# Down-projection: FFN rows loaded from POOL's queue, and the residual added by accumulating DMAs

## The chip, the cores and the metric

The kernel runs on one core of one Trainium2 chip. The metric is the device time of one execution in microseconds; the time before is the median of three runs. The engines are PE (TensorE matmul), DVE (VectorE), ACT (ScalarE), POOL (GpSimd) and SP (SyncE, which only issues DMAs here). Each engine works through its own instructions in the order in which the built program holds them, and waits on semaphores of the others.

## The reference

One step of a decoder layer on 1024 prompt positions and 8 sample tokens, that is 1032 columns in the kernel's layout. Only the end of it bears on the change:

```python
h = x + merged @ w_out
up = rmsnorm(h, norm_ffn) @ w_up
...
gate, val = jnp.split(c, 2, axis=-1)
h = h + (jax.nn.gelu(gate) * val) @ w_down
...
y_prompt = rmsnorm(h_p, norm_final)
y_sample = rmsnorm(h_s, norm_final)
```

`w_down` is 2816 x 1024, so the contraction of the down-projection has 22 row blocks of 128 (`NFF = 22`) and its output has 8 row blocks of 128 (`KT = 8`).

## The kernel before

Everything lies feature by position: a tile has 128 features as partitions and 1032 positions as columns. Matmuls are fp32 by splitting: each operand is a rounded part (`hi`) and a rest (`lo`), and three matmuls (hi x hi, hi x lo, lo x hi) make one product. Casts of the rounded part stand on ACT, the differences on DVE.

**Up-projection.** For each f of 22, `up_unit(f)` (L1263 on) computes two row blocks, `ff_rows(f)` applies the convolution, the gelu and the product and stores the result, g of f, to a scratch tensor `g_d[f]` in device memory from SP's queue (L1324). The residual h was stored to `hT_d` long before.

**Loading a row of g.** `load_g(f, after)` (L1334) makes one FFN row ready for the down-projection. It takes a buffer `gt`; `touch` (L92) copies one element into it on DVE, which ties the load to whatever `after` names; the DMA (L1337) loads 516 KB from SP's queue; ACT casts `gh` (L1340); DVE forms `gl` (L1341).

**Down-projection.** The 22 rows are taken in groups of 4, 5, 5, 5 and 3 (`DOWN_GROUPS`). For each of the first four groups, `down` (L1366) runs over the eight output row blocks j, and for each j over three blocks of columns (384, 384, 264). One such block is a chain of three matmuls per f in one PSUM bank; then `post` evicts it: DVE adds the sum to `hT[j]` (tile name `hD`, L1372). While `wide[0]` is not None, `mmtile` deals the blocks to two PSUM pools of four banks each in turn, so eight banks hold sums that are being made or that wait for their eviction. `hT[j]` before the first group is the residual: `load_h` loads the eight tiles from POOL's queue (L1351), in two steps that run in the last up-projection unit behind the loads of the first group's rows.

**What sets the order.** Steps that are to run beside matmuls are closures in a list `side`; each contraction step calls `tick`, which pops one. The loads of a following group are such steps, each with an `idle` between: while group n is multiplied, the rows of group n+1 are loaded. The language's scheduler then fixes the order of the instructions on each engine when the program is built; nothing moves at run time.

The last group of three rows (`last_down`) and the final normalisation follow; the change does not touch them.

Of the kernel before, what the change touches and what calls it, by code (L numbers as in the profile page):

```python
# [9 lines left out]
F32 = mybir.dt.float32  # L10
# [3 lines left out]
ALU = mybir.AluOpType  # L14
# [6 lines left out]
KT = 8  # L21
S = 1024
NS = 8
T = S + NS
DFF = 2816
NFF = DFF // P
# [18 lines left out]
def kernel(  # L45
# [8 lines left out]
    nc = tc.nc  # L54
# [14 lines left out]
    def uid(s):  # L69
        counter[0] += 1  # L70
        return f"{s}_{counter[0]}"

    def ftile(name, dt=F32):
        return fpool.tile([P, FCOLS], dt, tag="f", name=uid(name))
# [10 lines left out]
    def xtile(name):  # L85
        return pxx.tile([P, 512], F32, tag="xx", name=uid(name))
# [4 lines left out]
    def touch(dst, src):  # L91
        nc.vector.tensor_copy(dst[0:1, 0:1], src[0:1, 0:1])  # L92
# [62 lines left out]
    side = deque()  # L155
# [13 lines left out]
    def drain():  # L169
        while side:  # L170
            side.popleft()()


    def load_raw(w2d, r0, nk, c0):
        raw = wpool.tile([P, KT, P], F32, tag="wraw", name=uid("wraw"))
        nc.sync.dma_start(
            raw[:, :nk, :],
            w2d[r0:r0 + nk * P, c0:c0 + P].rearrange("(k p) c -> p k c", p=P),
        )
        return raw  # L180
# [10 lines left out]
    def split_w(raw, nk):  # L191
        parts = [split_part(raw[:, k:min(k + 4, nk), :]) for k in range(0, nk, 4)]
        hi = [parts[k // 4][0][:, k % 4, :] for k in range(nk)]
        lo = [parts[k // 4][1][:, k % 4, :] for k in range(nk)]
        return hi, lo

    def load_w(w2d, r0, nk, c0):

        return split_w(load_raw(w2d, r0, nk, c0), nk)

    def unit(w, src, nk, post, b, blocks):

        hi, lo = w
        t0, n = blocks[b]
        ps = mmtile("mm")
        for k in range(nk):
            xh, xl = src(k, t0, n)
            nc.tensor.matmul(ps[:, :n], hi[k], xh, start=(k == 0), stop=False)  # L208
            nc.tensor.matmul(ps[:, :n], hi[k], xl, start=False, stop=False)  # L209
            nc.tensor.matmul(ps[:, :n], lo[k], xh, start=False, stop=(k == nk - 1))  # L210
            if k < nk - 1:
                tick(1 / nk)
        post(b, t0, n, ps)
        tick(1 / nk)
# [16 lines left out]
    def dense(w, ahi, alo, post, tbs=(0, 1, 2), blocks=TB):  # L231
        def src(k, t0, n):
            return ahi[k][:, t0:t0 + n], alo[k][:, t0:t0 + n]

        for b in tbs:
            unit(w, src, len(ahi), post, b, blocks)
# [891 lines left out]
    for hp in range(2):  # L1128
        bh = ftile("bh", F32R)
        bl = ftile("bl", F32R)  # L1130
        for hf in range(2):
            ps = xtile("bps")
            for j in range(4):
                nc.tensor.transpose(ps[:, j * P:(j + 1) * P], oA[hp][:, hf * 4 + j, :], ident)
            cs = slice(hf * 512, hf * 512 + 512)
# [27 lines left out]
    for p in range(2):  # L1163
        t0, n = HALF[p]
        for i in range(4):
            h = ftile("hT")
# [5 lines left out]
    hT_d = dpool.tile([KT, P, T], F32, tag="hT_d", name="hT_d")  # L1172
    g_d = dpool.tile([NFF, P, T], F32, tag="g_d", name="g_d")
# [83 lines left out]
    ups = {}  # L1257
# [5 lines left out]
    def up_unit(f):  # L1263

        wa, wb = up_weights(f)
        ups[f] = [ftile("up") for _ in range(2)]
        for up in ups[f]:
            nc.gpsimd.memset(up[:, 0:2], 0.0)

        def outs(p):  # L1270
            t0, n = HALF[p]
            return [up[:, 2 + t0:2 + t0 + 2 * n] for up in ups[f]]

        pair_unit(wa, wb, hn, outs)
# [41 lines left out]
    def ff_rows(f, t0=0, t1=T):  # L1316
        ug, uv = ups.pop(f)
        n = t1 - t0
        cg, cv = (ftile("cv") for _ in range(2))
        conv(f, ug, cg, t0, t1)  # L1320
        nc.scalar.activation(cg[:, :n], cg[:, :n], AF.Gelu_apprx_tanh)
        conv(f + NFF, uv, cv, t0, t1)
        nc.vector.tensor_tensor(cg[:, :n], cg[:, :n], cv[:, :n], op=ALU.mult)
        nc.sync.dma_start(g_d[f][:, t0:t1], cg[:, :n])  # L1324

    for p in range(2):
        t0, n = HALF[p]
# [6 lines left out]
    def load_g(f, after):  # L1334
        gt = ftile("gt")
        touch(gt, after)
        nc.sync.dma_start(gt[:, :T], g_d[f])  # L1337
        gh = ftile("gh", F32R)
        gl = ftile("gl", F32R)
        nc.scalar.copy(gh[:, :T], gt[:, :T])  # L1340
        nc.vector.tensor_tensor(gl[:, :T], gt[:, :T], gh[:, :T].bitcast(F32), op=ALU.subtract)  # L1341
        return gh, gl

    hT = []
    gs = []

    def load_h(js):
        for j in js:
            h = ftile("hD")
            touch(h, ups[NFF - 1][0][:, 2:3])  # L1350
            nc.gpsimd.dma_start(h[:, :T], hT_d[j])  # L1351
            hT.append(h)

    for f in range(EARLY, NFF):
        if f == NFF - 1:
            side.append(idle)
            for i in range(DOWN_GROUPS[0]):
                side.append(lambda i=i: gs.append(load_g(i, ups[NFF - 1][0][:, 2:3])))
            side.append(lambda: load_h(range(4)))
            side.append(lambda: load_h(range(4, KT)))  # L1360
        up_unit(f)
        drain()
        ff_rows(f)


    def down(f0, gs):  # L1366
        for j in range(KT):
            w = load_w(w_down[0], f0 * P, len(gs), j * P)

            def post(b, t0, n, ps, j=j):  # L1370
                cs = slice(t0, t0 + n)
                nc.vector.tensor_tensor(hT[j][:, cs], ps[:, :n], hT[j][:, cs], op=ALU.add)  # L1372

            dense(w, [a for a, _ in gs], [a for _, a in gs], post)

    wide[0] = 0
    f0 = 0
    for size, following in zip(DOWN_GROUPS, DOWN_GROUPS[1:]):
        nxt = []
        for f in range(f0 + size, f0 + size + following):  # L1380
            side.append(idle)
            side.append(lambda f=f: nxt.append(load_g(f, hT[0])))
        down(f0, gs)
        drain()
        f0, gs = f0 + size, nxt
# [4 lines left out]
    for q in range(5):  # L1390
        ps = xtile("cop")
# [14 lines left out]
    f0, gs = pend  # L1406
# [130 lines left out]
```

## Time and profile before

| what | us |
|---|---|
| median of 3 runs | 1525.52 (1525.44 to 1526.32) |
| the profiled execution's own time | 1525.51 |
| its span, first to last instruction | 1523.8 |
| PE busy in it | 1500.1 (98%) |
| DVE busy | 901.1 (59%) |
| ACT busy | 590.2 (39%) |
| POOL busy | 114.3 (7%) |
| mean granted clock of PE | 0.996 of full |

The profiled execution lies 1.7 us over its span (what stands ahead of the first and behind the last instruction), and 0.01 us from the median. Busy time is summed over an engine's instructions; a matmul's recorded end overlaps the next one's start. "Idle before, releaser" is the time that an engine stood still just before an instruction, and what ended it. Times in the views are microseconds from the start of the span.

### The profile page before, as it was taken

To read this page: it belongs to the slowest core of one execution; us is meant where nothing else is said; L and a number is where in the kernel's file an instruction comes from. 1 tells how busy PE (TensorE), PEld (TensorE's weight loads), DVE (VectorE), ACT (ScalarE), POOL (GpSimd) and SP (SyncE) were. 2 spreads that over 40 slices of the span, in tenths; PEclk is the share of its full clock that TensorE was granted. 3 is DMA by queue.
4 is the path that set the end of the run, shared out by engine and by line. 5 is a ranking of instruction groups with operands and counts; after the bars stand their busy time and mean duration, and the time that the engine had idled before them with its cause. 6 is when DMAs were issued, how large, how long until landed. Compare 5 with 4: busy or idle time off the path is not lost.

```text
span 1523.8 us, 25982 instructions
## 1 busy us (share of the span) xinstructions
PE 1500.1 (98%) x10518; PEld 1435.9 (94%) x10518; DVE 901.1 (59%) x1768; ACT 590.2 (39%) x1223; POOL 114.3 (7%) x275
## 2 busy tenths in 40 slices
PE   7999999999999999999999999999999999999997
PEld 7988999899999799998899999999999999899997
DVE  5444435435757224545687887878788856534436
ACT  6444333344121212333456655444445542212114
POOL 1100123132000200002000300000000001000000
PEclk9999999999999999999999999999999999999999
DMA  8300122133116311126443322222222246423302
GB/s 253 117 19 29 54 73 79 46 83 107 36 39 187 101 40 49 39 59 204 143 140 105 91 67 74 84 83 72 83 84 84 77 127 216 119 75 90 117 22 112
DMA packets 169420, 140.11 MB, mean 92 GB/s; under 512 B 7394, under 2 KB 154053, under 8 KB 169293
## 3 DMA queue, kind: packets, MB, share of 16 engines
q1 hardware_dynamic: 160277, 115.41, 25.0%
q0 software_dynamic: 8992, 23.04, 5.0%
q8 instruction: 82, 1.34, 0.4%
q14 instruction: 37, 0.30, 0.1%
q10 hardware_dynamic: 32, 0.01, 0.0%
HBM read 107.97 MB, written 30.68 MB: 91 GB/s over the span
## 4 chain that ended last, share of the span: by engine, by line
PE 94%; DMA 3%; DVE 2%; ACT 1%; issue 1%; SPq 0%; ACTq 0%; DVEq 0%
PE mm L208 19%; PE mm L209 19%; PE mm L210 19%; PE mm L277 8%; PE mm L275 8%; PE mm L278 8%; PE s L561 2%; PE po L586 2%; PE pt L576 1%; DMA gt<-g_d 1%; DMA x<-in_x_prompt_dram 1%; PE mm L711 1%; PE pv L871 1%; PE mm L713 1%; PE mm L712 1%; PE mm L1420 1%
## 5 line engine op out<-in xcount | busy, mean ns | idle before, releaser
L187 ACT CAST whi<-wraw 128x512 fp32r<-128x512 f32 (+2 forms) x275 | 158.4, 586 | 390.8 <-PE mm L209 281.1
L208 PE MATMUL mm<-xnh,whi 128*128 128x384 f32 (+3 forms) x936 | 308.6, 330 | 0.0
L277 PE MATMUL mm<-xc,whi 128*128 128x256 f32 (+1 forms) x1064 | 300.4, 282 | 0.0
L278 PE MATMUL mm<-xc,wlo 128*128 128x256 f32 (+1 forms) x1064 | 300.3, 282 | 0.0
L275 PE MATMUL mm<-xc,whi 128*128 128x256 f32 (+1 forms) x1064 | 300.2, 282 | 0.0
L210 PE MATMUL mm<-xnh,wlo 128*128 128x384 f32 (+3 forms) x936 | 299.6, 320 | 0.0
L209 PE MATMUL mm<-xnl,whi 128*128 128x384 f32 (+3 forms) x936 | 299.6, 320 | 0.0
L188 DVE TENSOR_TENSOR wlo<-wraw,whi 128x512 fp32r<-128x512 f32 (+2 forms) x275 | 174.2, 643 | 71.4 <-ACT whi L187 67.6
L277 PEld LDWEIGHTS mm<-xc,whi 128*128 128x128 f32 x1064 | 201.2, 189 | 0.0
L275 PEld LDWEIGHTS mm<-xc,whi 128*128 128x128 f32 x1064 | 201.1, 189 | 0.0
L278 PEld LDWEIGHTS mm<-xc,wlo 128*128 128x128 f32 x1064 | 200.8, 189 | 0.0
L208 PEld LDWEIGHTS mm<-xnh,whi 128*128 128x128 f32 x936 | 176.1, 188 | 12.3 <-issue 6.8
L209 PEld LDWEIGHTS mm<-xnl,whi 128*128 128x128 f32 x936 | 176.2, 188 | 3.7 <-issue 0.7
L210 PEld LDWEIGHTS mm<-xnh,wlo 128*128 128x128 f32 x936 | 175.9, 188 | 3.6 <-issue 0.7
L208 PE MATMUL mm<-gh,whi 128*128 128x384 f32 (+1 forms) x456 | 146.2, 322 | 4.7 <-ACT gh L1340 4.7
L209 PE MATMUL mm<-gl,whi 128*128 128x384 f32 (+1 forms) x456 | 147.3, 323 | 0.9 <-DVE gl L1341 0.8
L210 PE MATMUL mm<-gh,wlo 128*128 128x384 f32 (+1 forms) x456 | 146.4, 321 | 0.0
L1372 DVE TENSOR_TENSOR hD<-mm,hD 128x384 f32<-128x384 f32 (+1 forms) x96 | 48.0, 509 | 84.5 <-PE mm L210 84.3
L1312 DVE SCALAR_TENSOR_TENSOR cv<-up,cw,cv 128x1024 f32<-128x1024 f32 x76 | 97.1, 1278 | 0.8 <-issue 0.8
L208 PEld LDWEIGHTS mm<-gh,whi 128*128 128x128 f32 x456 | 86.4, 190 | 5.5 <-ACT gh L1340 5.5
L187 ACT CAST whi<-ws 128x512 fp32r<-128x512 f32 x76 | 47.2, 621 | 108.6 <-PE mm L277 107.4
L209 PEld LDWEIGHTS mm<-gl,whi 128*128 128x128 f32 x456 | 86.7, 190 | 1.7 <-DVE gl L1341 1.1
(295 smaller groups left out, 2599.0 us busy)
## 6 DMA issues: line engine op xcount, KB each, us to landing
wraw<-in_w_up_dram SPq DMA_DIRECT2D x50, 512.0 KB
wraw<-in_w_in_dram SPq DMA_DIRECT2D x42, 512.0 KB
gt<-g_d SPq DMA_DIRECT2D x22, 516.0 KB
g_d<-cv SPq DMA_DIRECT2D x19, 516.0 KB
wraw<-in_w_out_dram SPq DMA_DIRECT2D x16, 512.0 KB
wraw<-in_w_down_dram SPq DMA_DIRECT2D x24, 320.0 KB
xT_d<-xT POOLq DMA_DIRECT2D x8, 516.0 KB, 5.3
hD<-hT_d POOLq DMA_DIRECT2D x8, 516.0 KB, 7.4
```

What stands on the lines that cost most here:

```text
L187: nc.scalar.copy(hi[:, :n, :], src)
L188: nc.vector.tensor_tensor(lo[:, :n, :], src, hi[:, :n, :].bitcast(F32), op=ALU.subtract)
L208: nc.tensor.matmul(ps[:, :n], hi[k], xh, start=(k == 0), stop=False)
L209: nc.tensor.matmul(ps[:, :n], hi[k], xl, start=False, stop=False)
L210: nc.tensor.matmul(ps[:, :n], lo[k], xh, start=False, stop=(k == nk - 1))
L275: nc.tensor.matmul(ps, hi[:, k, :], xh, start=(first and k == 0), stop=False, skip_group_check=not first)
L277: nc.tensor.matmul(ps, hi[:, k, :], xl, start=False, stop=False, skip_group_check=not first)
L278: nc.tensor.matmul(ps, lo[:, k, :], xh, start=False, stop=(k == 3), skip_group_check=not first)
L561: nc.tensor.matmul(ps[:, off:off + ncol], qf[hr, qc:qc + P], kf[hr, kc:kc + ncol], start=True, stop=True)
L586: nc.tensor.matmul(po[:, gi * 64:gi * 64 + 64], pt[:, j * P:(j + 1) * P], vt[:, n, 64 * h:64 * h + 64], start=(bi == 0), stop=(bi == nb - 1))
L1312: nc.vector.scalar_tensor_tensor(c[:, :m], up[:, i:i + m], wi, c[:, :m], op0=ALU.mult, op1=ALU.add)
L1372: nc.vector.tensor_tensor(hT[j][:, cs], ps[:, :n], hT[j][:, cs], op=ALU.add)
```

## The change

The rows of g are loaded from POOL's queue in place of SP's. `load_h` is gone: in the first group, whose eviction made the sum `hD + PSUM` on DVE, ACT now copies the PSUM block into a fresh `hD` tile, and behind the three copies of each j a DMA on POOL's queue adds `hT_d[j]` to it (`accum_op=ALU.add`). Later groups add on DVE as before. The touch of a following group's load reads `gh` of the current group's first row (`gs[0][0]`) in place of `hT[0]`.

```diff
@@ -1334,7 +1334,7 @@
     def load_g(f, after):
         gt = ftile("gt")
         touch(gt, after)
-        nc.sync.dma_start(gt[:, :T], g_d[f])
+        nc.gpsimd.dma_start(gt[:, :T], g_d[f])
@@ -1344,20 +1344,11 @@
-    def load_h(js):
-        for j in js:
-            h = ftile("hD")
-            touch(h, ups[NFF - 1][0][:, 2:3])
-            nc.gpsimd.dma_start(h[:, :T], hT_d[j])
-            hT.append(h)
-
     for f in range(EARLY, NFF):
         if f == NFF - 1:
             side.append(idle)
             for i in range(DOWN_GROUPS[0]):
                 side.append(lambda i=i: gs.append(load_g(i, ups[NFF - 1][0][:, 2:3])))
-            side.append(lambda: load_h(range(4)))
-            side.append(lambda: load_h(range(4, KT)))
@@ -1366,12 +1357,19 @@
     def down(f0, gs):
         for j in range(KT):
             w = load_w(w_down[0], f0 * P, len(gs), j * P)
+            if f0 == 0:
+                hT.append(ftile("hD"))
 
             def post(b, t0, n, ps, j=j):
                 cs = slice(t0, t0 + n)
-                nc.vector.tensor_tensor(hT[j][:, cs], ps[:, :n], hT[j][:, cs], op=ALU.add)
+                if f0 == 0:
+                    nc.scalar.copy(hT[j][:, cs], ps[:, :n])
+                else:
+                    nc.vector.tensor_tensor(hT[j][:, cs], ps[:, :n], hT[j][:, cs], op=ALU.add)
 
             dense(w, [a for a, _ in gs], [a for _, a in gs], post)
+            if f0 == 0:
+                nc.gpsimd.dma_start(hT[j][:, :T], hT_d[j], accum_op=ALU.add)
@@ -1379,7 +1377,7 @@
-            side.append(lambda f=f: nxt.append(load_g(f, hT[0])))
+            side.append(lambda f=f, after=gs[0][0].bitcast(F32): nxt.append(load_g(f, after)))
```

How the built program's order changes is shown at three places. In the rows, numbers only tell tiles apart. In the program before, gt_13593, 13634, 13669, 13710 and 13751 are the second group's rows f = 4 to 8; in the changed one they are gt_13570, 13613, 13648, 13691 and 13734, and hD_13551, 13608, 13672 and 13729 are `hT[0]` to `hT[3]`.

ACT while the first group is multiplied, before: casts of the second group's rows (gh of f = 4 to 7) alternate with casts of weights.

```order
L1340 CAST gh_13596<-gt_13593 128x1032
L187 CAST whi_13994<-wraw_13988 128x128
L1340 CAST gh_13637<-gt_13634 128x1032
L187 CAST whi_14058<-wraw_14056 128x512
L1340 CAST gh_13672<-gt_13669 128x1032
L187 CAST whi_14062<-wraw_14056 128x128
L1340 CAST gh_13713<-gt_13710 128x1032
L187 CAST whi_14133<-wraw_14131 128x512
```

The same place in the changed program, from gh of f = 4 to gh of f = 7.

```order
L1340 CAST gh_13573<-gt_13570 128x1032
L1340 CAST gh_13616<-gt_13613 128x1032
L1366 COPY hD_13608<-mm_13609 128x384
L1366 COPY hD_13608<-mm_13630 128x384
L1366 COPY hD_13608<-mm_13644 128x264
L187 CAST whi_13986<-wraw_13980 128x128
L1340 CAST gh_13651<-gt_13648 128x1032
L1366 COPY hD_13672<-mm_13673 128x384
L1366 COPY hD_13672<-mm_13687 128x384
L1366 COPY hD_13672<-mm_13708 128x264
L187 CAST whi_14050<-wraw_14048 128x512
L1340 CAST gh_13694<-gt_13691 128x1032
```

The first group's evictions of j = 1 now stand on ACT behind gh of f = 4 and f = 5, those of j = 2 behind gh of f = 6; those of j = 3 follow gh of f = 7 and f = 8. The copies of j = 0 stand ahead of these rows, and those of j = 4 to 7 follow j = 3 with no gh between.

POOL's queue from the last row of the first group (f = 3) on, in the changed program; before, it held only the eight loads of hD here.

```order
L1337 DMA gt_13446<-g_d 128x1032
L1372 DMA hD_13551<-hT_d 128x1032
L1337 DMA gt_13570<-g_d 128x1032
L1337 DMA gt_13613<-g_d 128x1032
L1372 DMA hD_13608<-hT_d 128x1032
L1337 DMA gt_13648<-g_d 128x1032
L1372 DMA hD_13672<-hT_d 128x1032
L1337 DMA gt_13691<-g_d 128x1032
L1337 DMA gt_13734<-g_d 128x1032
L1372 DMA hD_13729<-hT_d 128x1032
```

The loads of f = 4, 6 and 7 each stand directly behind an accumulating DMA, which itself waits for ACT's three copies of that j.

DVE where the second group's rows are prepared, in the changed program: L92 is the touch ahead of a load, L1341 forms gl.

```order
L92 COPY gt_13570<-gh_13331 1x1
L188 TENSOR_TENSOR wlo_13883<-wraw_13880,whi_13882 128x512
L1323 TENSOR_TENSOR cv_13528<-cv_13528,cv_13529 128x1032
L188 TENSOR_TENSOR wlo_13933<-wraw_13930,whi_13932 128x512
L188 TENSOR_TENSOR wlo_13983<-wraw_13980,whi_13982 128x512
L1341 TENSOR_TENSOR gl_13574<-gt_13570,gh_13573 128x1032
L92 COPY gt_13613<-gh_13331 1x1
L1341 TENSOR_TENSOR gl_13617<-gt_13613,gh_13616 128x1032
L92 COPY gt_13648<-gh_13331 1x1
L188 TENSOR_TENSOR wlo_13987<-wraw_13980,whi_13986 128x128
L1341 TENSOR_TENSOR gl_13652<-gt_13648,gh_13651 128x1032
L92 COPY gt_13691<-gh_13331 1x1
```

The first group's additions to hD no longer stand among these rows; each touch still stands behind gl of the row ahead of it, as it did before.

## Rows read from the trace of the kernel before

**Rows 1.** The page: busy us of each engine, share of the span, instructions.

```profile
PE 1500.1 (98%) x10518; PEld 1435.9 (94%) x10518; DVE 901.1 (59%) x1768; ACT 590.2 (39%) x1223; POOL 114.3 (7%) x275
```

**Rows 2.** Stretches: length, busy per engine (instructions), PE clock, DMA share, GB/s.

```profile
1246.00:1256.00 10.00, 7.87 (x40) 7.20 (x40) 2.68 (x5) 1.85 (x3) 0.60 (x1) 0.83 0.60 189
1256.00:1297.00 41.00, 41.00 (x263) 40.69 (x262) 25.50 (x55) 11.84 (x15) 4.20 (x8) 1.00 0.58 201
1297.00:1307.00 10.00, 6.49 (x28) 5.91 (x27) 3.76 (x9) 1.25 (x2) 0.00 (x0) 0.83 0.43 123
1307.00:1471.00 164.00, 164.00 (x1045) 164.00 (x1044) 71.15 (x142) 32.62 (x59) 0.53 (x1) 1.00 0.30 89
```

**Rows 3.** PE's waits from 1200 us on: total us, times, longest us.

```profile
PE mm L208 <- ACT gh L1340: 4.7, 2, 2.7
PE mm L209 <- DVE gl L1341: 0.8, 1, 0.8
```

**Rows 4.** Timeline of PE, start and length in us, idle before in brackets.

```profile
1246.65 0.34 PE L208 MATMUL mm<-gh,whi 128*128 128x384 f32 x1
...
1249.91 0.62 PE L208 MATMUL mm<-gh,whi 128*128 128x384 f32 x2 [2.04 <-ACT gh L1340]
...
1254.64 0.28 PE L208 MATMUL mm<-gh,whi 128*128 128x264 f32 x1
1254.76 0.28 PE L209 MATMUL mm<-gl,whi 128*128 128x264 f32 x1
...
1255.01 0.34 PE L208 MATMUL mm<-gh,whi 128*128 128x384 f32 x1
...
1257.10 1.09 PE L208 MATMUL mm<-gh,whi 128*128 128x384 f32 x5
```

**Rows 5.** Timeline of SP, loads of f = 3, 4 and 5.

```profile
1251.20 0.34 SPq L1337 DMA_DIRECT2D gt<-g_d  x1
...
1266.36 0.39 SPq L1337 DMA_DIRECT2D gt<-g_d  x1
...
1278.38 0.34 SPq L1337 DMA_DIRECT2D gt<-g_d  x1
```

**Rows 6.** Timeline of ACT, casts of the same three rows.

```profile
1256.17 1.05 ACT L1340 CAST gh<-gt 128x1032 fp32r<-128x1032 f32 x1 [5.51 <-DMA gt<-g_d]
...
1275.93 1.06 ACT L1340 CAST gh<-gt 128x1032 fp32r<-128x1032 f32 x1 [7.35 <-DMA gt<-g_d]
...
1281.96 1.06 ACT L1340 CAST gh<-gt 128x1032 fp32r<-128x1032 f32 x1 [4.78 <-DMA gt<-g_d]
```

**Rows 7.** Timeline of DVE between the first group's last row and f = 6.

```profile
1258.41 0.56 DVE L92 COPY hD<-up 1x1 f32<-1x1 f32 x8
1258.89 1.26 DVE L1312 SCALAR_TENSOR_TENSOR cv<-up,cw,cv 128x1024 f32<-128x1024 f32 x1
...
1264.22 0.54 DVE L1372 TENSOR_TENSOR hD<-mm,hD 128x384 f32<-128x384 f32 x1
...
1278.17 0.13 DVE L92 COPY gt<-hD 1x1 f32<-1x1 f32 x1
...
1283.06 1.23 DVE L1341 TENSOR_TENSOR gl<-gt,gh 128x1032 fp32r<-128x1032 f32 x1 [2.68 <-ACT gh L1340]
1284.21 0.13 DVE L92 COPY gt<-hD 1x1 f32<-1x1 f32 x1
```

**Rows 8.** hD's loads on POOL: issue in ns, and issue to landing (min/median/max).

```profile
L1351 POOL DMA_DIRECT2D hD<-hT_d x8: 527/528/536, 1259.1 to 1263.0; - x8
...
DMA to landing us min/median/max: 3.7/7.4/13.1
```

**Rows 9.** DMA issues: a lone transfer on POOL's queue, size, us to landing.

```profile
out_dram<-in_state_conv_ffn_dram POOLq DMA_DIRECT2D x1, 176.0 KB, 8.7
```

**Rows 10.** ACT's copies out of PSUM by shape: busy us, mean ns.

```profile
L389 ACT COPY xT<-xps 128x384 f32<-128x384 f32 x8 | 3.7, 471 | 2.6 <-PE xps L381 2.6
L284 ACT COPY up<-mm 128x260 f32<-128x260 f32 x19 | 7.0, 370 | 0.0
```

## The prediction

> **What bounds the kernel now.** I read the page first: PE is busy for 98% of the span [rows 1], so only what makes PE wait, or slows it, can move the time. Then the stretches of the down-projection [rows 2]: PE is full in 1256 to 1297 and in 1307 to 1471, and idle for 2.1 us in 1246 to 1256 and 3.5 us in 1297 to 1307. In each of these two pieces of 10 us the granted clock is 0.83: behind the idle time PE runs at the lower of its two levels for a while, which costs 0.17 x 10 = 1.7 us a time. So this stage holds 2.1 + 3.5 + 2 x 1.7 = 9.0 us that a better order could give back, and no more. PE's waits say what for [rows 3]: for gh and gl, the two halves of a loaded FFN row. The first wait is at the third row of the first group, 2.04 us [rows 4]; the second, inside 1297 to 1307, is for the last row of the second group.
>
> Rows come one at a time. A touch on DVE stands behind the gl of the row before it, so a step is: touch, 0.2 us to the DMA's issue, the load, 1.06 us of cast, 1.23 us of difference. For f = 5: touch at 1278.17, issue at 1278.38, cast at 1281.96, next touch at 1284.21 [rows 5 to 7]. From issue to cast (call it L) that is 3.6 us, and the rest of the step is 1284.21 - 1278.17 - 3.58 = 2.46 us. L was 5.0 us for f = 3, with weight loads beside it, and 9.6 us for f = 4 [rows 5, 6], while the eight loads of hD, issued from 1259.1 to 1263.0, were landing [rows 8]. Those 6 us are why the second group's last row is late.
>
> **What the change removes.** The hD loads go, and with them f = 4's long landing: the second stall, 3.5 + 1.7 = 5.2 us, can go. It does, since by the working below the second group's last row is ready some 12 us before PE reaches that group. The 96 additions on DVE become 72, and 24 copies go to ACT, 0.47 us for 384 columns and 0.37 for 264 [rows 10]; neither engine's busy time is near the bound. SP loses 22 issues; PE's waits name none of its weights [rows 3], so that gains nothing.
>
> **What it adds at the first group.** A load on POOL alone takes 3.7 us to land, and 0.1 to the cast: L = 3.8 against 3.6 on SP. Such a load also no longer stands ahead of the weights in SP's queue; f = 3, with weights beside it, needed 5.0. I take +0.3 a row (ends 0 and 1.0), nearest to the load alone. PE's first stall waits for the third row: 2.0 becomes 2.9, so +0.9.
>
> The Trainium skill's page "SBUF — State Buffer" (the box on the "DVE blocks DMA" trap) says that a DMA issued from GpSimd can stand still while VectorE holds the port that both share, and advises the other queues. The rows do not show it here: eight issues on POOL took 527 to 536 ns each [rows 8] while DVE worked without a break from 1258.9 to 1264.2 [rows 7]. By that rule each load would lose up to the 1.2 us of a DVE instruction, some 9 us over these eight rows, and the time would be 1550, inside the range below; by the rows nothing, and the sum counts nothing.
>
> **What it adds behind that: evictions queue behind casts.** This is the main term. ACT's new order puts the copies of j = 1 behind gh of f = 4 and 5, those of j = 2 behind gh of f = 6, those of j = 3 behind gh of f = 7 and 8. Each gh waits for a load. While ACT waits there, finished sums stay in PSUM, and PE owns eight banks: with j = 0 evicted it can go on for eight blocks, to the end of block 11, and no further. Twelve matmuls of 384 columns take 1257.10 - 1255.01 = 2.09 us, twelve of 264 take 12 x 0.12 = 1.44 [rows 4]; a j of three blocks takes 5.6, and 11 blocks take 21.0.
>
> PE starts the group at 1246.65, so it is out of banks at 1246.65 + 21.0 + 2.9 + 1.7 = 1272.3.
>
> Now the chain. gl of f = 3 ended at 1258.4 and DVE then worked on the convolution for 5.3 us [rows 7]; with 4 x 0.3 more, f = 4's touch is at 1264.9. Its load stands behind the first accumulating DMA, issued some 2.5 us earlier.
>
> No row shows an accumulating DMA. From below it costs what a plain load of hD does, which it is in size, queue, source and target; from above I take the slowest lone transfer on this queue, 8.7 us [rows 9]. I take near the first, as the nearest row: it holds up a load right behind it by 1.9 us, which is the pace of the eight plain loads (from the first landing at 1262.8 to the last at 1276.1, seven steps), so L = 3.8 + 1.9 = 5.7; for f = 4, 2.5 us later, half, so L = 4.8.
>
> **Stall A.** f = 5's touch: 1264.9 + 4.8 + 2.46 = 1272.2. Its cast ends at 1272.2 + 0.2 + 3.8 + 1.06 = 1277.3, the first copy of j = 1 at 1277.7. PE waits 1277.7 - 1272.3 = 5.4, and 1.7 of clock: 7.1 us.
>
> **Stall B.** Three banks come free: PE runs 5.6 + 1.7 = 7.3 us, to 1285.0. f = 6's load stands behind the accumulating DMA of j = 1, which needs all three copies (1278.6): its load starts at 1279.3, its cast ends at 1286.1, the first copy of j = 2 at 1286.5. Wait 1.5; the rows show no fall of the clock behind so short a wait, so none is counted.
>
> **Stall C.** PE runs 5.6 us, to 1292.1. f = 7's load stands behind j = 2's accumulating DMA: start 1288.1, cast ends 1294.9, gl and f = 8's touch at 1296.0, f = 8's cast ends at 1301.1, the first copy of j = 3 at 1301.5. Wait 9.4, clock 1.7: 11.1 us. Behind that no gh stands between copies, PE has seven blocks (some 13 us) left in the group, and every row of the next is there.
>
> **Sum.** +0.9 - 5.2 + 7.1 + 1.5 + 11.1 = +15.4 us. The profiled execution took 1525.51, the median is 1525.52; so 1541 us, 1.0% slower.
>
> **Ends.** With L = 3.5 for every load and a free accumulating DMA, the same steps give A 3.5 + 1.7, B 0, C 6.0 + 1.7, first stall unchanged: +7.7, so 1533. With 8.7 us of landing for each accumulating DMA, f = 4 loses 2.4 more and f = 6 and 7 lose 4.3 each, and B is then long enough for 1.7 of clock: +15.4 + 12.7 = 1553.6; I add 4 for loads on POOL at +1.0 a row: 1558.
>
> **The rivals.**
> (1) The accumulating DMAs are dearer than any row suggests, and POOL's queue becomes the bound: at the 13.1 us of hD's longest landing [rows 8] each, f = 4, 6 and 7 lose 6.8, 8.2 and 8.2 us against the forecast, and with 1.7 of clock that is 1541 + 24.9 = 1566, more where the last five, issued together, also delay the third group's rows. For it: no price is known, and all 22 row loads share that queue. Against: a plain load of the same tile lands in 3.7 us. The page "DMA: Bandwidth & Descriptors" of the Trainium skill (Queues, rings and completion order) says that a DMA engine takes turns between queues and works through one queue's ring in order; by that a row loaded from SP would share time with an accumulating DMA, where on POOL's queue it stands behind the whole of it. No run here shows that yet.
> (2) Faster: the loads keep ahead of PE's banks, A, B and C vanish, and only the second stall's end is left: 1525.5 - 5.2 + 0.9 = 1521. It decides at f = 5's cast: that would have to end by 1271.8, 6.9 us behind f = 4's touch, so that two loads would need 6.9 - 2.46 - 0.2 - 1.06 = 3.2 us together. The shortest single one here took 3.6. I give it little.
> (3) Even: the stalls come, but at about 5 us in all, as much as the removed one: 1525. It needs A without C, that is, f = 7 and 8 loaded in one step's time, against a touch that still stands behind each gl.
>
> **How the numbers follow.** A measurement of this kernel can tell about 0.2%, 3 us, from no change. Forecast 0.80 (1533 to 1558), dear accumulating DMAs 0.12 (above 1558), faster 0.04, even 0.04. So faster 0.04, same 0.04, slower 0.92. The range 1533 to 1558 is the forecast's own, with the two ends of the accumulating DMA in it; what it leaves out is 2 in 10.
>
> **What would show it.** In the profile after: PE idle in the first group for a bank, so a matmul of L208 behind ACT's copy (L1366), twice for over 3 us, near 1272 and 1292; ACT's gh of f = 5 and f = 8 idle for a DMA just before copies of hD; no wait of PE near the second group's start; clock below 1.00 behind each long wait; DVE's additions of the later groups as before. If PE never waits for L1366, the main term is wrong; if the accumulating DMAs land in over 9 us, its size is; a PE wait inside 1307 to 1471 in later groups would be a cost that I count as nothing.

## The result, and the profile after

The changed kernel takes 1547.15 us (median of 4 runs, 1545.71 to 1551.62), the kernel before, beside it on the same chip, 1525.92 us (1525.44 to 1526.74): a ratio of the means of 1.0142, 95% interval 1.0124 to 1.0161. The forecast was 1541 us, the range 1533 to 1558. The profiled execution took 1546.65 us with a span of 1544.9, that is 21.1 us over the span before.

The page, busy time by engine. It answers to [rows 1]: PE's share falls by one point, DVE has 13 us less, ACT 9 us more, and neither is near a bound.

```profile
PE 1504.8 (97%) x10518; PEld 1440.2 (93%) x10518; DVE 887.7 (57%) x1736; ACT 598.8 (39%) x1247; POOL 129.1 (8%) x297
```

Stretches of the down-projection, with the columns of [rows 2].

```profile
1246.00:1256.00 10.00, 6.13 (x34) 5.81 (x33) 3.87 (x7) 2.46 (x5) 1.60 (x3) 0.89 0.44 117
1256.00:1270.00 14.00, 14.00 (x88) 14.00 (x87) 9.04 (x13) 7.14 (x10) 1.45 (x2) 0.96 0.46 103
1270.00:1282.00 12.00, 5.74 (x31) 5.42 (x30) 3.26 (x5) 3.22 (x6) 1.65 (x3) 0.82 0.46 154
1282.00:1295.00 13.00, 10.68 (x51) 10.36 (x51) 2.27 (x4) 3.01 (x6) 1.72 (x3) 0.77 0.64 134
1295.00:1310.00 15.00, 6.68 (x32) 6.36 (x31) 2.81 (x4) 5.55 (x12) 2.58 (x4) 0.72 0.37 96
1310.00:1330.00 20.00, 20.00 (x123) 20.00 (x123) 3.77 (x8) 4.45 (x9) 3.41 (x5) 0.96 0.94 205
1330.00:1492.00 162.00, 160.98 (x1020) 160.35 (x1019) 66.48 (x138) 30.87 (x58) 6.34 (x12) 1.00 0.29 87
```

In the 84 us from 1246 to 1330 PE is busy for 63.2 and idle for 20.8; in the kernel before it was idle for 5.6 in the same stage (2.1 and 3.5, [rows 2]). Besides the first stall there are holes where the three stalls A, B and C were forecast, in 1270 to 1282, 1282 to 1295 and 1295 to 1310, and all lie in the first group.

PE's waits from 1200 us on (total us, times, longest us), to be read against [rows 3].

```profile
PE mm L208 <- ACT hD L1366: 16.9, 3, 8.3
PE mm L208 <- ACT gh L1340: 3.9, 1, 3.9
PE mm L210 <- DVE wlo L188: 1.0, 2, 0.6
```

The first line is new: a first matmul of a block waits for ACT's copy out of PSUM. It comes three times. The second is the first stall, 3.9 in place of 2.0; the second stall of the kernel before, for gh and gl of the second group's last row, is gone; the third line is 1.0 us in a later group (near 1407 and 1415). The second stall is not gone because rows come sooner: f = 8, the last of them, is cast at 1304.51 (below) where in the kernel before it was cast at 1299.87. PE, held up by the stalls ahead of it, comes to the second group later still.

The timeline of PE, the four idle times.

```profile
1252.87 0.75 PE L208 MATMUL mm<-gh,whi 128*128 128x384 f32 x3 [3.87 <-ACT gh L1340]
1279.97 0.59 PE L208 MATMUL mm<-gh,whi 128*128 128x264 f32 x1 [6.26 <-ACT hD L1366]
1290.22 0.39 PE L208 MATMUL mm<-gh,whi 128*128 128x264 f32 x1 [2.33 <-ACT hD L1366]
1306.00 0.59 PE L208 MATMUL mm<-gh,whi 128*128 128x264 f32 x1 [8.32 <-ACT hD L1366]
```

The timeline of ACT says why the copies come so late.

```profile
1272.10 1.06 ACT L1340 CAST gh<-gt 128x1032 fp32r<-128x1032 f32 x1 [2.02 <-DMA gt<-g_d]
1278.49 1.05 ACT L1340 CAST gh<-gt 128x1032 fp32r<-128x1032 f32 x1 [5.33 <-DMA gt<-g_d]
1279.45 1.13 ACT L1366 COPY hD<-mm 128x384 f32<-128x384 f32 x3
...
1288.73 1.05 ACT L1340 CAST gh<-gt 128x1032 fp32r<-128x1032 f32 x1 [5.64 <-DMA gt<-g_d]
1289.69 1.13 ACT L1366 COPY hD<-mm 128x384 f32<-128x384 f32 x3
...
1297.82 1.05 ACT L1340 CAST gh<-gt 128x1032 fp32r<-128x1032 f32 x1 [5.03 <-DMA gt<-g_d]
1304.51 1.05 ACT L1340 CAST gh<-gt 128x1032 fp32r<-128x1032 f32 x1 [5.64 <-DMA gt<-g_d]
1305.47 2.94 ACT L1366 COPY hD<-mm 128x384 f32<-128x384 f32 x8
```

Before every run of copies stands a cast that waited about 5.5 us for a load. The last line, eight copies in a row, is a queue: eight sums, one for each bank, that had been finished before. PE resumes 0.5 us after the first copy starts, each time.

Stretches behind each of PE's idle times, from where it works again at the lower clock to where the full clock is back.

```profile
1252.87:1257.17 4.30, 4.30 (x18) 4.30 (x19) 1.27 (x2) 0.00 (x0) 0.53 (x1) 0.60 0.29 63
1279.97:1284.46 4.49, 4.49 (x18) 4.49 (x19) 1.18 (x3) 0.91 (x3) 1.44 (x2) 0.50 0.46 62
1291.29:1294.70 3.41, 3.41 (x14) 3.41 (x13) 0.69 (x1) 0.62 (x1) 1.23 (x2) 0.50 0.63 86
1306.00:1311.77 5.77, 5.77 (x22) 5.77 (x23) 1.12 (x2) 3.02 (x9) 2.62 (x3) 0.50 0.57 97
```

PE is busy throughout them and runs at the lower of its two levels (0.50) for all or most of the time, so they cost 1.7, 2.2, 1.7 and 2.9 us (length times what the clock lacks of 1.00), 8.5 together; before it was twice 1.7. **The account:** PE's idle time grew by 20.8 - 5.6 + 1.0 = 16.2 us, the slow pieces by 8.5 - 3.4 = 5.1, which makes 21.3 where the span grew by 21.1.

The account adds up idle time and slow time; it does not say that each stall costs its own length. What ends A, B and C is the chain of rows, and from A on the chain waits for PE nowhere: each run of copies above goes through without a break, and each cast ahead of one waits for a load. What PE lost at A and B would otherwise have been waited for at C. So the time should follow the moment at which PE resumes behind C, and it does in the four kernels that have C: 1306.00 here (span 1544.9 us), 1305.68 with the copies on DVE (1543.8), 1302.25 with plain DMAs (1539.6), 1297.02 with the rows on SP (1533.2). The spans differ by somewhat more than these moments, since the shorter ones also have less slow time behind C or no wait in a later group.

Last, the accumulating DMAs (issue in ns min/median/max; then us from issue to landing), the term that had no row before. The plain loads of the kernel before are in [rows 8].

```profile
L1372 POOL DMA_DIRECT2D hD<-hT_d x8: 853/877/896, 1263.6 to 1322.4; - x8
...
DMA to landing us min/median/max: 5.4/6.1/8.5
```

### The profile page after: what moved, and what is told of

Its sections match the earlier page's. It is cut to its first block, busy times and chain, and to the rows that moved or that the text cites. A ratio compares the mean times of both kernels' runs of the same rounds, so it can differ in the third digit from the quotient of the medians.

```text
span 1544.9 us, 25981 instructions
## 1 busy us (share of the span) xinstructions
PE 1504.8 (97%) x10518; PEld 1440.2 (93%) x10518; DVE 887.7 (57%) x1736; ACT 598.8 (39%) x1247; POOL 129.1 (8%) x297
## 5 line engine op out<-in xcount | busy, mean ns | idle before, releaser
L208 PE MATMUL mm<-gh,whi 128*128 128x384 f32 (+1 forms) x456 | 148.7, 328 | 20.8 <-ACT hD L1366 16.9
L210 PEld LDWEIGHTS mm<-gh,wlo 128*128 128x128 f32 x456 | 88.9, 195 | 1.7 <-DVE wlo L188 1.7
```

## The experiments

Theory 1 is the prediction's: in the first group ACT's order puts evictions behind casts that wait for loads, and PE runs out of PSUM banks. Its rivals: theory 2, the accumulating DMAs on POOL's queue are the price by themselves; theory 3, the loads moved to POOL are. Ratios are to the kernel before, measured on the same chip.

| kernel | median us | ratio, 95% interval | PE's waits for copies of hD |
|---|---|---|---|
| the change | 1547.15 | 1.0142 (1.0124 to 1.0161) | 16.9 us, 3 |
| change, gh of f >= 4 on DVE | 1526.77 | 1.0006 (0.9995 to 1.0017) | none |
| change, plain DMA | 1542.09 | 1.0107 (1.0090 to 1.0124) | 15.0, 3 |
| change, rows on SP | 1535.22 | 1.0057 (1.0041 to 1.0074) | 9.6, 2 |
| change, copies on DVE | 1546.99 | 1.0137 (1.0121 to 1.0153) | 17.1, 2 |
| change, loads one step ahead | 1522.19 | 0.9977 (0.9967 to 0.9986) | none |
| before, rows on POOL | 1528.47 | 1.0019 (1.0009 to 1.0028) | none |
| before, new touch alone | 1519.80 | 0.9957 (0.9942 to 0.9972) | none |
| before, loads one step ahead | 1519.00 | 0.9952 (0.9938 to 0.9967) | none |
| before, all loads ahead | 1515.30 | 0.9929 (0.9916 to 0.9943) | none |
| change, all loads ahead | 1515.44 | 0.9930 (0.9917 to 0.9942) | none |

### Casts out of ACT's way

```diff
-        nc.scalar.copy(gh[:, :T], gt[:, :T])
+        if f < DOWN_GROUPS[0]:
+            nc.scalar.copy(gh[:, :T], gt[:, :T])
+        else:
+            nc.vector.tensor_copy(gh[:, :T], gt[:, :T])
```

> The changed kernel with one line more: the casts gh of rows f = 4 and later stand on DVE, so that ACT's copies of the first group's sums no longer stand behind an instruction that waits for a load. Loads, queues and accumulating DMAs stay. Theory 1 (order on ACT: evictions behind waiting casts, PE out of banks): PE's wait for ACT's copies, 16.9 us in the changed kernel, falls under 2 us, and the three half-clock pieces behind it, 6.8 us of lost pace, go too: 1547 - 16.9 - 6.8 = 1523. DVE pays: a step of a row grows by up to a cast there (a difference of that size takes 1.23 us), so rows of the second group can come late by up to 5 x 1.2 us and the time reach 1530. Theory 2 (the accumulating DMAs and POOL's queue are the price, whatever ACT does): the loads land as late as in the changed kernel, and the time stays within 5 us of 1547.

1526.77 us, inside theory 1's 1523 to 1530; single runs went from 1522.86 to 1531.38. PE's waits, in the profiled execution, which was the fastest of the ten:

```profile
PE mm L208 <- ACT gh L1341: 3.2, 1, 3.2
PE mm L210 <- DVE wlo L188: 1.2, 1, 1.2
PE mm L209 <- DVE gl L1344: 0.8, 1, 0.8
PE mm L208 <- DVE gh L1343: 0.4, 1, 0.4
```

No wait for a copy is left, though the loads of f = 4 to 8 on POOL still stand among accumulating DMAs, and these now land in 5.6/8.6/14.1 us, later than in the changed kernel. About 20 of the 21 us hang on what ACT does between the evictions. What remains is the first stall and 2.4 us of waits for operands that DVE, with the casts on it, finishes late.

### The accumulation taken out

```diff
-                nc.gpsimd.dma_start(hT[j][:, :T], hT_d[j], accum_op=ALU.add)
+                nc.gpsimd.dma_start(hT[j][:, :T], hT_d[j])
```

> The changed kernel with a plain DMA in place of the accumulating one: the first group's sums are overwritten with the residual, so that part of the output leaves the first four rows' products out. Order on every engine, issues and bytes stay. Theory 1: ACT still holds the copies behind gh, so the stalls stay; only what an accumulating DMA costs more than a plain one goes (issue 0.88 against 0.53 us; landing 5.4 to 6.1 against 3.7), for f = 4, 6 and 7, which stand behind one each: 3 x 2 us, so 1547 - 6 = 1541 (1538 to 1545), and PE still waits for L1366 for over 8 us in all. Theory 2: the stalls go with the accumulation, 1523 to 1528, and PE waits for L1366 for under 3 us.

1542.09, within theory 1's 1538 to 1545: the accumulation is worth some 5 us of the 21. (The first group's sums are overwritten in this kernel; it serves for its time alone.) A and C stand, with 6.70 and 8.18 us; B, last line below, is all but gone:

```profile
PE mm L208 <- ACT hD L1366: 15.0, 3, 8.2
...
1288.18 0.39 PE L208 MATMUL mm<-gh,whi 128*128 128x264 f32 x1 [0.16 <-ACT hD L1366]
```

The saving is at the loads directly behind a DMA of hD: from the load's issue to its cast f = 6 took 4.7 us (1281.96 to 1286.70) where it took 7.3 behind an accumulating one (1281.46 to 1288.73), and f = 7 took 4.5 (1289.66 to 1294.13) for 6.1. f = 4, whose load comes 3.2 us behind one, gained nothing (5.8 for 5.3), which the expectation's "3 x 2 us" had wrong. PE resumes behind C 3.75 us sooner, and the 1.0 us of waits in a later group is gone.

### The rows back on SP

```diff
-        nc.gpsimd.dma_start(gt[:, :T], g_d[f])
+        nc.sync.dma_start(gt[:, :T], g_d[f])
```

> The changed kernel with the rows of g loaded from SP's queue again. Theory 1: the casts still wait for their loads with the copies behind them; what goes is the first stall's growth (3.9 back to 2.0 us) and what the loads of f = 4, 6 and 7 lost behind accumulating DMAs (about 2 us each), so 1547 - 2 - 6 = 1539 (1535 to 1544), with waits for L1366 of over 8 us in all. Theory 3 (POOL's queue for the loads is what costs): the time returns to 1523 to 1528.

1535.22, in theory 1's range at its lower end; theory 3's is missed by 7 us. The middle stall is gone, the outer two are smaller:

```profile
PE mm L208 <- ACT hD L1366: 9.6, 2, 6.1
PE mm L208 <- ACT gh L1340: 2.2, 2, 1.8
```

So the queue doesn't make the stalls, but it decides how long they are: on SP the issues of the first group's rows stand 6.0 to 6.8 us apart, on POOL 7.1 to 7.7, and f = 7's load, issued at 1285.45, beside an accumulating DMA issued at 1285.39, reached its cast at 1289.67, after 4.2 us, where behind such a DMA on POOL's queue f = 6 and 7 took 7.3 and 6.1. (What the runs give back overlaps and does not add up: 20 us with the casts off ACT, 5 with plain DMAs, 12 with the rows on SP, of 21 in all.)

### The rows on POOL in the kernel before

The same line the other way round, in the kernel before.

> The kernel before with one part of the change alone: the rows of g loaded from POOL's queue. Evictions stay additions on DVE, the residual is loaded by plain DMAs. Theory 1 (evictions behind casts that wait are the price, queue and accumulation a small part): the first stall grows from 2.0 to about 3.5 us and the loads of f = 4 and 5 stand behind the eight loads of hD on one queue, so the second stall, 3.5 us before, can grow by some 3 us; no wait for a bank. 1525.5 + 1.5 + 3 = 1530 (1525 to 1534). Theory 3 (POOL's queue for the loads makes most of the loss): 1538 or more.

1528.47, within theory 1's 1525 to 1534. PE's waits:

```profile
PE mm L208 <- ACT gh L1340: 6.2, 2, 3.1
```

The first stall is 3.1 us long, the second 3.1 too: the second did not grow as expected, though f = 4's load now stands behind all of hD's on one queue (issue 1268.87, cast 1277.86). The move to POOL alone costs 2.5 us; the same move on top of the other parts of the change costs 1547.15 - 1535.22 = 12. The difference is that, there, evictions stand behind these loads.

### The copies on DVE

```diff
-                    nc.scalar.copy(hT[j][:, cs], ps[:, :n])
+                    nc.vector.tensor_copy(hT[j][:, cs], ps[:, :n])
```

> The changed kernel with the first group's sums copied on DVE in place of ACT, all else as changed. In DVE's new order the copies of j = 1 stand behind gl of f = 4 and 5, those of j = 2 and 3 behind gl of f = 6 to 8, and each gl waits for the same loads as gh. Theory 1 (what counts is that a copy stands behind an instruction that waits for a load, on whichever engine): three stalls as in the changed kernel, now for DVE's copies, each a difference (1.2 us) later or some loads sooner: 1540 to 1552, waits for DVE's copies of over 12 us. Rival 4 (ACT is the wrong engine for evictions, DVE evicts in time as it did before): 1523 to 1528.

1546.99, as in the changed kernel. Waits of PE, and the timeline of DVE around the stalls:

```profile
PE mm L208 <- DVE hD L1366: 17.1, 2, 8.9
```

```profile
1281.50 1.23 DVE L1341 TENSOR_TENSOR gl<-gt,gh 128x1032 fp32r<-128x1032 f32 x1 [5.12 <-ACT gh L1340]
1282.65 1.01 DVE L1366 COPY hD<-mm 128x384 f32<-128x384 f32 x2
...
1303.92 1.23 DVE L1341 TENSOR_TENSOR gl<-gt,gh 128x1032 fp32r<-128x1032 f32 x1 [5.26 <-ACT gh L1340]
1305.07 4.08 DVE L1366 COPY hD<-mm 128x384 f32<-128x384 f32 x9
```

The pattern is that of ACT, one engine on: a gl that waited for its cast, and the cast for its row, and behind it a queue of copies. ACT is not the wrong engine for evictions; the place behind a late row is the wrong place. (There are two stalls here and not the three expected: in this order f = 6's load stands ahead of j = 1's accumulating DMA on POOL's queue and is cast after 4.4 us, 1284.24 to 1288.65, so that j = 2's copies come soon enough.)

### The new touch alone

```diff
-            side.append(lambda f=f: nxt.append(load_g(f, hT[0])))
+            side.append(lambda f=f, after=gs[0][0].bitcast(F32): nxt.append(load_g(f, after)))
```

> The kernel before with the smallest part of the change alone: a following row's touch names gh of the group's first row in place of hT[0], which the first group's DVE additions write. Theory 1: f = 4's touch no longer stands behind the first addition of j = 0 (1264.2 us), but the loads of hD still land until 1276, so f = 4's load stays long and the second stall shrinks by at most 3 us: 1522 to 1526. A rival, that the touch is what moves the casts ahead of the evictions: 1535 or more.

1519.80: faster than the range expected. The second stall is not smaller, it is gone; one wait of 1.7 us is left. The touch of f = 4 no longer waits for the addition that writes hT[0]. Timeline of DVE (touch of f = 4), then of ACT (casts of f = 4 and 5):

```profile
1259.74 0.13 DVE L92 COPY gt<-gh 1x1 f32<-1x1 f32 x1
```

```profile
1264.70 1.04 ACT L1340 CAST gh<-gt 128x1032 fp32r<-128x1032 f32 x1
1277.30 1.06 ACT L1340 CAST gh<-gt 128x1032 fp32r<-128x1032 f32 x1 [7.84 <-DMA gt<-g_d]
```

f = 4's load left at 1259.94, with the first of hD's, and was cast at 1264.70 where before it was 1275.93 [rows 6]. The expectation held that f = 4 would be long among hD's loads in any case; instead f = 5 is the long one (8.4 us from its issue at 1268.90), and the casts of f = 5 to 8 come 4.4 to 4.7 us earlier than before, enough for the second group. So one of the change's lines is worth -6 us by itself, and it was there to be had without the rest. Within the change it earns nothing of the kind: there f = 4's touch comes at 1266.15, behind the convolution on DVE, where before it came at 1265.83.

### Loads issued one step ahead

In both kernels `load_g` is cut in two, `fetch` (touch and load) and `halves` (cast and difference), and a following group's steps become:

```diff
-        for f in range(f0 + size, f0 + size + following):
+        raw = []
+        nextf = range(f0 + size, f0 + size + following)
+        for i in range(following + 1):
             side.append(idle)
-            side.append(lambda f=f, after=gs[0][0].bitcast(F32): nxt.append(load_g(f, after)))
+            if i < following:
+                side.append(lambda f=nextf[i], after=gs[0][0].bitcast(F32): raw.append(fetch(f, after)))
+            if i >= 1:
+                side.append(lambda i=i - 1: nxt.append(halves(raw[i])))
```

In the changed kernel:

> The changed kernel with a following group's touch and load issued one step ahead of the cast and the difference of the row before it, so that a load has a step's time to land before ACT comes to its cast; evictions on ACT, accumulating DMAs and POOL's queue stay. Theory 1: ACT's copies may stand behind gh as before, but gh no longer waits, so stalls A, B and C go with their clock: 1547 - 16.9 - 6.8 = 1523, the first stall of 3.9 us left as it is (1519 to 1528). Theory 2: the accumulating DMAs are all there and on the same queue, with the loads behind them, so at least two of the three stalls stay, and the time is 1538 or more.

1522.19, as theory 1 has it (1519 to 1528), with every accumulating DMA in place on the same queue. They land later than before the repair, 5.3/8.3/10.9 us, and PE never waits for a copy:

```profile
PE mm L208 <- ACT gh L1343: 4.0, 1, 4.0
```

The timeline of ACT is worth a look, since the casts still wait, and copies stand behind them:

```profile
1282.84 1.05 ACT L1343 CAST gh<-gt 128x1032 fp32r<-128x1032 f32 x1 [4.51 <-DMA gt<-g_d]
1283.80 0.85 ACT L1372 COPY hD<-mm 128x384 f32<-128x384 f32 x2
1286.96 1.06 ACT L1343 CAST gh<-gt 128x1032 fp32r<-128x1032 f32 x1 [2.31 <-DMA gt<-g_d]
1287.93 0.37 ACT L1372 COPY hD<-mm 128x264 f32<-128x264 f32 x1
```

No run of blocks piles up behind one cast here: the waits are shorter, and there are copies between every two casts. A wait ahead of an eviction costs nothing as long as the free banks last over it. This repair shortens the waits and reorders the copies at once, so it doesn't say how much is due to which; no kernel kept the order and took the waits alone away.

In the kernel before (with `hT[0]` as the touch's source):

> The kernel before with a following row's touch and load issued one step ahead of the cast and the difference of the row before it. Theory 1 (rows come one at a time because each touch stands behind the gl of the row ahead): the second stall goes with its clock, 3.5 + 1.7 = 5.2 us; the first group's loads are not touched, so the first stall stays: 1525.5 - 5.2 = 1520 (1518 to 1523). If f = 4's long landing among hD's loads is the limit whatever the order, the second stall stays and the time is 1524 to 1527.

1519.00: the second stall is gone, and only the first is left (2.1 us), as forecast.

### The first group's rows ahead as well

On top of each of these two, the first group's rows are fetched two steps ahead of their casts:

```diff
-            for i in range(DOWN_GROUPS[0]):
-                side.append(lambda i=i: gs.append(load_g(i, ups[NFF - 1][0][:, 2:3])))
+            first = []
+            for i in range(DOWN_GROUPS[0] + 2):
+                if i < DOWN_GROUPS[0]:
+                    side.append(lambda i=i: first.append(fetch(i, ups[NFF - 1][0][:, 2:3])))
+                if i >= 2:
+                    side.append(lambda i=i - 2: gs.append(halves(first[i])))
```

> The kernel before, with following rows loaded one step ahead as in the run before that had this, and the first group's rows two steps ahead of their casts as well. Theory 1 (each stall is a row whose load was issued behind the difference of the row ahead): the first stall, 2.07 us, and its 1.7 us of clock go too: 1519.0 - 3.8 = 1515 (1514 to 1518), with no wait of PE over 0.5 us in the four groups. If the first group's rows are late because the last product rows are stored late, the stall stays, and the time is 1518 to 1520.

> The changed kernel (evictions copied on ACT, accumulating DMAs, loads on POOL) with following rows loaded one step ahead and the first group's rows two steps ahead of their casts. Theory 1: the first stall of 4.0 us goes with its clock, in which 10 + 14 us ran at 0.79 and 0.91 of the clock, 3.4 us: 1522.2 - 4.0 - 3.4 = 1515 (1514 to 1519), as fast as the kernel before with the same repair within 0.2%. If an ACT eviction or an accumulating DMA has a price of its own on the path, it stays over 3 us slower than that one.

1515.30 and 1515.44: both beat the kernel before by 0.7%, and they can't be told apart. Of PE's waits one line is left in either, 0.2 us in the final normalisation, and the stretches of the changed kernel with this repair read:

```profile
1246.00:1256.00 10.00, 9.90 (x65) 9.58 (x64) 9.95 (x16) 7.99 (x13) 0.78 (x2) 1.00 0.30 82
1256.00:1480.00 224.00, 224.00 (x1418) 223.71 (x1417) 88.45 (x175) 50.10 (x99) 17.03 (x27) 1.00 0.39 110
```

PE is full at the full clock from 1256 to 1480. ACT's evictions, the accumulating DMAs (5.4/8.4/8.7 us to land) and POOL's queue show no price of their own on the path once the rows come early: what they cost in the change was paid through rows that came late.

## Why the prediction was right

| term | forecast us | measured us |
|---|---|---|
| first stall grows | +0.9 | 3.87 - 2.04 = +1.8 |
| second stall goes | -3.5 - 1.7 | -3.5 - 1.7 |
| stall A, idle and clock | 5.4 + 1.7 | 6.26 + 2.2 |
| stall B | 1.5 + 0 | 2.33 + 1.7 |
| stall C | 9.4 + 1.7 | 8.32 + 2.9 |
| later groups | 0 | +1.0 |
| sum | +15.4 | +21.3 (the span: +21.1) |

**The main term** holds: three waits for a bank, for L1366, at 1273.7, 1287.9 and 1297.7 where 1272.3, 1285.0 and 1292.1 were forecast, each behind a cast that waits for a load. The runs with gh on DVE and with loads ahead remove it and with it the whole loss; the run with copies on DVE makes it again elsewhere. Working out when PE is out of banks, from the length of a block, and then when the next eviction can come, from the step of a row, gave A's idle time to within 1 us. That C agrees to 0.1 us with its clock is luck: its idle time was forecast 1.1 us too long and its slow time 1.2 too short. That the second stall goes was right too, by the prediction's own reason that PE comes to the second group long after its last row. But it was put down to the loads of hD, and the runs do not bear that out: the touch alone, and the loads one step ahead, each remove it with hD's loads in place, and in the change the rows come later than before, so the -5.2 is no gain of the change but a wait that A, B and C take the place of.

**Rivals.** (1), the dear accumulating DMAs, fell: they land in 5.4 to 8.5 us, under the 9 that would have spoken against the size, and taking the accumulation out gives back 5 us. What the Trainium skill's page "DMA: Bandwidth & Descriptors" (Queues, rings and completion order) says of turns between queues, and of the order within one, agrees with the run with rows on SP: 4.2 us beside an accumulating DMA against 6.1 and 7.3 behind one. (2), faster, and (3), even, fell with A and C. The port rule of the Trainium skill's page "SBUF — State Buffer" (the "DVE blocks DMA" trap), which the prediction priced at 1550 and didn't count, is stated there for DVE instructions in a 2-port mode, a condition that the prediction left out. The measured 1547 is nearer to 1550 than to 1541, so the time by itself doesn't speak against it. The issues do: the trace of the change has 22 of rows, of 527 to 872 ns, median 530, the three above 0.8 us each directly behind an accumulating DMA's issue, and from touch to issue it took 0.66 us with DVE at work (1246.91 to 1247.57) and 0.67 with DVE idle (1254.00 to 1254.67). Not settled is what the loads themselves lost: from issue to cast f = 0 to 2 took 4.9, 4.5 and 4.2 us, where on SP they took 4.4, 3.8 and 3.8, and no run tells DVE's work from the weight loads beside them.

**What was mis-sized.** The sum was 6 us short. C ends at 1306.0 where 1301.5 was forecast (4.5 us), the slow time behind it is 1.2 longer, and later groups wait for 1.0; that is the 6 us to within 1. The terms behind it:
- "+0.3 a row (ends 0 and 1.0)" for a load on POOL. The touches of f = 0 to 3 came 7.73, 7.36 and 7.09 us apart, where before they were 6.85, 6.21 and 6.25: +0.96 a row, the upper end. About half of it stands between touch and issue, 0.66 us on POOL (1231.82 to 1232.48) against 0.20 on SP; a row for that was at hand in hD's own touches (1258.41, first issue 1259.1, [rows 7, 8]) and was not used.
- L = 5.7 behind an accumulating DMA. It was 7.3 for f = 6 and 6.1 for f = 7; without one it was 3.7 and 3.8 (f = 5 and 8), as forecast.
- "The rows show no fall of the clock behind so short a wait": behind B's 2.33 us of idle time PE ran 3.4 us at 0.50. The rows had it behind a wait not much longer, the first stall of 2.04 us in [rows 2], and the kernel with the new touch alone has it behind 1.69 us (a clock of 0.67 from 1250.37 to 1254.50). Behind A and C the lower level cost more than the 1.7 us counted, 2.2 and 2.9 us. Of these only what stands behind C lengthens the time; the rest made PE later at the next stall.

Against these, C was forecast 1.1 us too long in idle time: PE reached it later than forecast, so that less of the same lateness was left to wait for.

The forecast was short, then, since several small terms were each taken near their kind end. The nearest row for the accumulating DMA, a plain load, was too cheap: with plain DMAs in its place the kernel takes 1542.09, 1 us from the forecast (though there too its terms are off both ways: A 6.70 us idle for 5.4, B 0.16 for 1.5, C 8.18 for 9.4). And a term that repeats in a chain of steps weighs by the number of steps; its upper end belongs in the range as often as it repeats.

## What to carry to other kernels

Before an eviction is moved to an engine with time to spare, read what stands ahead of it in that engine's order and what that waits for: the engine's busy share (39% here) says nothing, the free PSUM banks times the length of a block is the time there is. Where rows come one at a time, because each load is issued only behind the last use of the row ahead, issue the loads a step or two early; with that repair the order of all that follows no longer mattered (1515.3 and 1515.4 us for the two kernels). And try the lines of a change one by one: of this one, the touch alone was a gain of 6 us, and the whole a loss of 21.

## What the runs showed of the hardware

- An accumulating DMA of 516 KB from POOL's queue took 853 to 896 ns to issue and 5.4 to 8.5 us to land; the plain one of the same size and target in its place took 527 to 530 ns and 3.7 to 5.0 us. A load issued right behind an accumulating one took 820 to 870 ns to issue where 530 is the median.
- The lower clock level began while PE stood idle, in the two longest stalls, and went on into the work behind. In A, PE did nothing from 1277.64 to 1279.97 at 0.50, and then 4.5 us of matmuls at the same level (lines below); in C the granted clock was 1.00 up to 1300 and 0.50 from 1302 on, and PE resumed at 1306.00.

```profile
1274.00:1277.60 3.60, 0.00 (x0) 0.00 (x0) 0.48 (x2) 0.00 (x0) 0.53 (x1) 1.00 0.39 116
1277.64:1279.97 2.33, 0.00 (x0) 0.00 (x0) 0.39 (x1) 1.48 (x3) 0.00 (x0) 0.50 0.11 44
```

- The cast of a 128x1032 row to the rounded part took 0.70 us on DVE (the run with gh there), 1.05 on ACT.
